# A gated feed-forward layer: the up-projection by a two-by-two Strassen scheme, the down-projection as a stage of its own

## The chip, the cores and the metric

The kernel runs on one core of one Trainium2 chip. The metric is device time in microseconds (us) of one execution, the median of several. The engines are named as in the profile: PE is TensorE (matrix products), PEld its weight load, DVE is VectorE, ACT is ScalarE, POOL is GpSimd, SP is SyncE, which here only issues DMAs; SPq is its queue.

## The reference

One layer of a streaming encoder: a token mixer, a cross-attention into 256 memory tokens and a gated feed-forward network, each with an RMS norm ahead and one behind, added to the residual. There are 2048 prompt rows and 64 sample rows, together T = 2112, and 1024 model columns. All is fp32. The change lies in the feed-forward part:

```python
def conv_ffn(xn, ff_buf, w_up, ffn_conv_w, w_down):
    up, ff_new = causal_dwconv(xn @ w_up, ff_buf, ffn_conv_w)   # width 3 along the rows
    a, g = jnp.split(up, 2, axis=-1)                            # 2 x 2816 columns
    return (jax.nn.gelu(g) * a) @ w_down, ff_new
...
    y = conv_ffn(rms_norm(x, p['norm_ffn_pre']), ff_buf, ...)
    x = x + rms_norm(y, p['norm_ffn_post'])
```

## The kernel before

Every fp32 operand of a product is split into a high part (a rounded copy, written by ScalarE, line 104) and a low part (value minus high part, a subtraction of two operands in SBUF on VectorE, line 105). A product of 128 rows of the contraction is then three matmuls into the same PSUM tile, high by high, high by low and low by high (`mm3`, lines 118 to 120).

The program has four phases. Phases 1 and 2 are the projections and the mixer, phase 3 the attention into the memory; it works through 16 chunks of 128 rows, ends each with a post-norm (`post`) and stores x2, the input of the feed-forward part, to DRAM. Phase 3 ends near 1473 us.

Phase 4 is the feed-forward part. It runs over four `BLOCKS` of rows: three of 512 and one of 512 + 64, which is handled as 2 x 288. In a block, `prep` loads x2, normalizes it and transposes it into SBUF, already split. Then come 22 pairs of up-projection tiles of 128 columns, one for the gate and one for the value: `up_tile` loads a weight tile of 1024 x 128, splits it, and runs 8 x 3 matmuls. VectorE then does the convolution straight from PSUM (lines 1313 to 1320), ScalarE the gelu, VectorE the gating product (line 1336) and the split of the gated rows, which stay in SBUF. The 22 tiles are cut into eight `PARTS`; after the up-projection of a part the down-projection of the part before it runs, its sums kept in SBUF (line 1384). So every weight of the up-projection is loaded and split four times, once per block. At the last part the two stores of the convolution state (`out_ffc`) are issued, and the last post-norms run.

The order of PE's instructions is the order of the code (`manual_schedule`); the order on the other engines is set by a scheduler, except for the tail, where it is written by hand as well. All loads go through SP's queue (`dma`), most stores of inner results through GpSimd's (`store`).

Of the kernel before, what the change touches and what calls it, by code (L numbers as in the profile page):

```python
# [14 lines left out]
P = 128  # L15
# [16 lines left out]
ZB = [("zh", 6144), ("zp", 1024), ("zy0", 1024), ("zy1", 1024), ("zy2", 1024), ("zy3", 1024), ("zy4", 1024),  # L32
      ("zc0", 1024), ("zc1", 1024), ("zc2", 1024), ("zc3", 1024)]
ZA = [("zx", 9216), ("za0", 1024), ("za1", 1024), ("za2", 1024), ("za3", 1024), ("za4", 1024), ("za5", 1024),
      ("za6", 1024)]
# [33 lines left out]
class Prog:  # L69
# [43 lines left out]
    def mm3(self, out, pairs, first=True, last=True):  # L113

        nc = self.nc
        n = len(pairs)
        for i, (lh, ll, rh, rl) in enumerate(pairs):
            nc.tensor.matmul(out, lhsT=lh, rhs=rh, start=(first and i == 0), stop=False)  # L118
            nc.tensor.matmul(out, lhsT=lh, rhs=rl, start=False, stop=False)  # L119
            nc.tensor.matmul(out, lhsT=ll, rhs=rh, start=False, stop=(last and i == n - 1))  # L120
# [17 lines left out]
    def build(self):  # L138
        tc, nc = self.tc, self.nc
        with ExitStack() as es:  # L140
# [21 lines left out]
            self.yaT = dt([4, P, T], F32, name="yaT")  # L162
            self.qT = dt([4, P, T], F32, name="qTd")
# [10 lines left out]
            self.zes = es  # L174
# [5 lines left out]
            self.phase4()  # L180

# [366 lines left out]
    def post(self, pool, halves, gb, xt, dst, w=P, tag="po", yn=None, junk=None, pl=False, hold=None):  # L548
# [9 lines left out]
        for i, h in enumerate(halves):  # L558
            (nc.gpsimd if pl else nc.vector).tensor_tensor(out=yn[:w, cut[i]], in0=h, in1=gb[:w, cut[i]], op=ALU.mult)
# [3 lines left out]
        def finish():  # L563
            for sl in cut:
                if pl:
                    nc.scalar.activation(yn[:w, sl], yn[:w, sl], AF.Copy, scale=r[:w, 0:1])
                    nc.gpsimd.tensor_tensor(out=yn[:w, sl], in0=yn[:w, sl], in1=xt[:w, sl], op=ALU.add)
                else:
                    nc.vector.scalar_tensor_tensor(out=yn[:w, sl], in0=yn[:w, sl], scalar=r[:w, 0:1], in1=xt[:w, sl],
                                                   op0=ALU.mult, op1=ALU.add)  # L570
# [406 lines left out]
    def phase3(self):  # L977
# [4 lines left out]
        zp = self.zp = self.pool(self.zes, "z")  # L982
        bt = [zp.tile([P, n], F32R, tag=t, name="B" + t) for t, n in ZB]
        at = [zp.tile([P, n], F32R, tag=t, name="A" + t) for t, n in ZA]

        def pieces(ts, sizes):
            return [t[:, i:i + D] for t, (_, n) in zip(ts, sizes) for i in range(0, n - D + 1, D)]
        bp, ap = pieces(bt, ZB), pieces(at, ZA)
        A = lambda part, k, sl: ap[part * KT + k][:, sl]
        B = lambda part, k, sl: bp[part * KT + k][:, sl]  # L990
        with ExitStack() as es:
# [67 lines left out]

            wk = self.pool(es, "p3k", side="right")  # L1060
# [16 lines left out]
            def xT(c):  # L1077
# [9 lines left out]
                t = wk.tile([P, 2, KT, P], F32R, tag="xs3", name="xs3", bufs=2)  # L1087
                if c:
                    s.x = wk.tile([P, D], F32, tag="x1", name="x1t", bufs=3)
                    self.dma(s.x, self.x1[c * P:(c + 1) * P])  # L1090
# [30 lines left out]

            def yout(s):
                yos = []
                for nh in range(2):
# [8 lines left out]
                    if nh == 1:  # L1133
                        self.post(wk, yos, self.gb3, s.x, self.x2[s.c * P:(s.c + 1) * P], yn=self.yn3,
                                  junk=s.pp[:, 0:2].rearrange("p h m -> p (h m)"))
                    yield

            self.up0 = []
# [5 lines left out]
            for i in range(16):  # L1144
# [4 lines left out]
                next(g, None)  # L1149
                if i + 2 < 16:  # L1150
                    ch[i + 2] = xT(i + 2)
                if i == 15:
                    for j in (NF, 0):
                        raw = self.raw(a["w_up"][j], (P, KT, P))
                        t = wk.tile([P, 2, KT, P], F32R, tag="xs3", name="up0", bufs=2)
                        self.split(t[:, 0], t[:, 1], raw)
                        self.up0.append((t[:, 0], t[:, 1]))
                if i == 14:
                    self.prep_open()
                    pg = self.prep(0, pt_, "tp")  # L1160
                y = yout(ch[i])
                next(y)
                if i == 15:
                    next(pg)
# [3 lines left out]
                if i >= 14:  # L1168
                    next(pg)
                next(y)  # L1170
                if i >= 14:
                    next(pg)
                if i == 15:
                    next(pg)
                next(y)
                if i == 14:
                    next(pg)
                    next(pg)
                if i == 1:
# [5 lines left out]
                              junk=ch[1].pp[:, 0:2].rearrange("p h m -> p (h m)"))  # L1185


    def prep_open(self):
        nc = self.nc
        zt = lambda t, n, dt=F32: self.zp.tile([P, n], dt, tag=t, name=t + "f")  # L1190
        self.x2s = zt("zx", 9216, F32R).rearrange("p (a k t) -> p a k t", a=2, k=KT)
        self.gpre = zt("za0", D)
        sl = [zt("za%d" % (i + 2), D) for i in range(4)]
        mis = zt("za6", D)
        self.halo = mis[:, 0:88].rearrange("p (j t) -> p j t", t=2)
        self.halos = mis[:, 88:176].rearrange("p (j t) -> p j t", t=2)
        self.ssx = mis[:, 176:240]
        self.flat = mis[:, 240:820]
        ex = zt("za1", D)
        xts = [sl[0], sl[1]]  # L1200
        xns = [sl[2], sl[3], ex]

        def slot(q):
            q.append(q.pop(0))
            return q[-1]

        def xn_slot():
            t = xns.pop(0)
            if t is not ex:
                xns.append(t)  # L1210
            return t
        self.xt_slot = lambda: slot(xts)
        self.xn_slot = xn_slot
        self.dma(self.gpre, self.a["g_ffnpre"].partition_broadcast(P))
        nc.vector.memset(self.halo, 0.0)
        self.dma(self.halos, self.a["sffn"])
        self.pc = 0

    def prep(self, b, pp, tag):

        nc = self.nc
        t0, npr, nsm = BLOCKS[b]
        n = npr + nsm
        xs = self.x2s

        def norm(s):
            w = min(P, n - s)
            xt, xn = self.xt_slot(), self.xn_slot()
            q = 4 * (self.pc % 8)
            self.pc += 1  # L1230
            ss, v, r = (self.ssx[:w, q + i:q + i + 1] for i in range(3))
            self.dma(xt[:w], self.x2[t0 + s:t0 + s + w])
            nc.scalar.activation(xn[:w], xt[:w], AF.Square, accum_out=ss)
            nc.vector.tensor_scalar(out=v, in0=ss, scalar1=1.0 / D, scalar2=EPS, op0=ALU.mult, op1=ALU.add)
            nc.gpsimd.tensor_tensor(out=r, in0=v, in1=self.mhalf[:w, 0:1], op=ALU.pow)
            nc.vector.scalar_tensor_tensor(out=xn[:w], in0=xt[:w], scalar=r, in1=self.gpre[:w], op0=ALU.mult, op1=ALU.mult)
            return xn, s, w
        todo = list(range(0, n, P))
        ready = [norm(todo.pop(0)), norm(todo.pop(0))]
        while ready:  # L1240
            xn, s, w = ready.pop(0)
            for h in range(2):
                tp = pp.tile([P, 4, P], F32, tag=tag, name="tp4")
                for k in range(4):
                    kk = 4 * h + k
                    nc.tensor.transpose(tp[:, k, :w], xn[:w, kk * P:(kk + 1) * P], self.ident[:w, :w])
                qs = slice(4 * h, 4 * h + 4)
                self.split(xs[:, 0, qs, s:s + w], xs[:, 1, qs, s:s + w], tp[:, :, :w])
                if h == 1 and todo:
                    ready.append(norm(todo.pop(0)))  # L1250
                yield

    def phase4(self):
        tc, nc, a = self.tc, self.nc, self.a
        V = nc.vector
        cst = self.cst
        with ExitStack() as es:
            wu = self.pool(es, "p4u", side="right")
            wd = self.pool(es, "p4d", side="right")
            ev = self.pool(es, "p4e", side="right")  # L1260
            xt_slot, xn_slot = self.xt_slot, self.xn_slot
            py = self.pool(es, "p4py", bufs=4, space=PSUM)
            pu = self.pool(es, "p4pu", bufs=4, space=PSUM)
            halo, halos = self.halo, self.halos
# [247 lines left out]
```

## Time and profile before

| | |
|---|---|
| median of 3 runs | 2996.48 us (2992.38 to 3001.1) |
| the profiled execution | 2998.96 us, its span 2997.3 us |
| mean granted TensorE clock | 0.995 |
| PE busy | 2943.8 us, 98% of the span, 15642 matmuls and transposes |
| VectorE busy | 1603.3 us, 53% |
| ScalarE busy | 1142.4 us, 38% |
| GpSimd busy | 242.3 us, 8% |
| chain that ended last | PE 92%, DMA 3%, VectorE 2%, ScalarE 1% |

The times are of whole executions; the span runs from the first to the last instruction that the trace records. The busy share is an average over all stages. The chain is followed back from the last instruction, at each step to what released it.

### The profile page before, as it was taken

What the parts mean: (1) busy time and instruction counts of PE and PEld (TensorE: products, weight loads), DVE (VectorE), ACT (ScalarE), POOL (GpSimd) and SP (SyncE); (2) the same over time, 40 slices, a digit from 0 to 9 for tenths busy, and PEclk for the clock granted to TensorE, in tenths of its full rate; (3) what the DMA queues carried; (4) which work ended last, traced back from release to release, by engine and by line L of the source; (5) the groups of instructions that cost most, each with busy time, mean ns of one, the idle gap of its engine ahead of it and who ended that gap; (6) DMA issues with size and microseconds to landing.
All of it is one profiled execution on the core that took longest, in us unless ns stands there. A gap on an engine that the chain in (4) does not pass through costs nothing.

```text
span 2997.3 us, 40249 instructions
## 1 busy us (share of the span) xinstructions
PE 2943.8 (98%) x15642; PEld 2605.3 (87%) x15642; DVE 1603.3 (53%) x2869; ACT 1142.4 (38%) x2402; POOL 242.3 (8%) x439
## 2 busy tenths in 40 slices
PE   8999999999999999999999999999999999999996
PEld 8999999998888878888788888888888888999995
DVE  6313421446666644333656567665676566655554
ACT  5233223224443432222443344433444334554342
POOL 1111111112212200000000000000000000000001
PEclk9999999999999999999999999999999999999998
DMA  8434332248666421111433235323353233322229
GB/s 275 145 98 134 97 114 88 63 150 297 208 216 194 134 74 60 43 42 50 155 106 106 91 100 162 105 92 106 99 169 107 91 106 102 131 92 85 78 85 54
DMA packets 145457, 352.26 MB, mean 118 GB/s; under 512 B 27094, under 2 KB 64152, under 8 KB 145266
## 3 DMA queue, kind: packets, MB, share of 16 engines
q1 hardware_dynamic: 129730, 299.36, 34.4%
q0 software_dynamic: 15536, 50.33, 4.3%
q8 instruction: 123, 2.02, 0.3%
q14 instruction: 68, 0.56, 0.1%
HBM read 296.60 MB, written 53.03 MB: 117 GB/s over the span
## 4 chain that ended last, share of the span: by engine, by line
PE 92%; DMA 3%; DVE 2%; ACT 1%; issue 1%; POOL 0%; SPq 0%; DVEq 0%; POOLq 0%; ACTq 0%
PE up L118 11%; PE up L120 11%; PE up L119 11%; PE y L118 5%; PE y L119 5%; PE y L120 5%; PE mm L119 4%; PE mm L120 4%; PE mm L118 4%; PE yo L118 3%; PE yo L119 3%; PE yo L120 3%; PE mmb L118 3%; PE mmb L120 3%; PE mmb L119 3%; PE sc L120 2%
## 5 line engine op out<-in xcount | busy, mean ns | idle before, releaser
L118 PE MATMUL up<-zxf,uh 128*128 128x512 f32 (+1 forms) x1744 | 612.0, 351 | 1.3 <-ACT uh L104 1.3
L120 PE MATMUL up<-zxf,ul 128*128 128x512 f32 (+1 forms) x1744 | 611.9, 351 | 0.0
L119 PE MATMUL up<-zxf,uh 128*128 128x512 f32 (+1 forms) x1744 | 611.8, 351 | 0.0
L105 DVE TENSOR_TENSOR ul<-raw,uh 128x1024 fp32r<-128x1024 f32 x174 | 213.1, 1225 | 360.4 <-ACT uh L104 360.4
L118 PEld LDWEIGHTS up<-zxf,uh 128*128 128x128 f32 x1744 | 327.2, 188 | 43.0 <-ACT uh L104 2.2
L120 PEld LDWEIGHTS up<-zxf,ul 128*128 128x128 f32 x1744 | 327.2, 188 | 40.8
L119 PEld LDWEIGHTS up<-zxf,uh 128*128 128x128 f32 x1744 | 327.2, 188 | 40.5
L118 PE MATMUL y<-dh,zhf 128*128 128x512 f32 x680 | 265.5, 390 | 0.0
L120 PE MATMUL y<-dh,zhf 128*128 128x512 f32 x680 | 264.9, 390 | 0.0
L119 PE MATMUL y<-dl,zhf 128*128 128x512 f32 x680 | 264.8, 389 | 0.0
L118 PE MATMUL mm<-xs,wh 128*128 128x384 f32 (+2 forms) x768 | 249.9, 326 | 9.5 <-ACT xs L110 7.4
L104 ACT CAST uh<-raw 128x1024 fp32r<-128x1024 f32 x174 | 183.0, 1052 | 194.5 <-PE up L119 193.5
L120 PE MATMUL mm<-xs,wl 128*128 128x384 f32 (+2 forms) x768 | 249.6, 325 | 0.7 <-DVE wl L105 0.6
L119 PE MATMUL mm<-xs,wh 128*128 128x384 f32 (+2 forms) x768 | 249.9, 326 | 0.0
L118 PE MATMUL mmb<-bh,xs 128*128 128x384 f32 (+1 forms) x512 | 173.4, 339 | 0.0
L120 PE MATMUL mmb<-bh,xs 128*128 128x384 f32 (+1 forms) x512 | 172.5, 337 | 0.0
L119 PE MATMUL mmb<-bl,xs 128*128 128x384 f32 (+1 forms) x512 | 172.4, 337 | 0.0
L104 ACT CAST dh<-raw 128x1024 fp32r<-128x1024 f32 x85 | 87.3, 1049 | 204.1 <-PE y L120 196.6
L118 PEld LDWEIGHTS mm<-xs,wh 128*128 128x128 f32 x768 | 146.4, 191 | 10.4 <-ACT xs L110 7.9
L120 PEld LDWEIGHTS y<-dh,zhf 128*128 128x128 f32 x680 | 127.6, 188 | 26.6
L118 PEld LDWEIGHTS y<-dh,zhf 128*128 128x128 f32 x680 | 127.7, 188 | 26.5 <-ACT za6f L1322 0.3
L119 PEld LDWEIGHTS y<-dl,zhf 128*128 128x128 f32 x680 | 127.7, 188 | 26.0
(514 smaller groups left out, 5537.8 us busy)
## 6 DMA issues: line engine op xcount, KB each, us to landing
raw<-in_w_up SPq DMA_DIRECT2D x176, 512.0 KB, 3.6
raw<-in_w_down SPq DMA_DIRECT2D x88, 512.0 KB, 3.6
raw<-in_wA SPq DMA_DIRECT2D x47, 512.0 KB, 3.7
xt<-in_x SPq DMA_DIRECT2D x32, 512.0 KB, 4.8
kvo_t<-kvo SPq DMA_DIRECT2D x16, 770.0 KB, 5.7
braw<-in_wB SPq DMA_DIRECT2D x64, 192.0 KB, 3.5
x1d<-yn POOLq DMA_DIRECT2D x16, 512.0 KB, 6.1
x2d<-yn POOLq DMA_DIRECT2D x16, 512.0 KB, 5.3
```

The source lines that it names most:

```text
L104: nc.scalar.copy(hi, src)
L105: (eng or nc.vector).tensor_tensor(out=lo, in0=src, in1=hi.bitcast(F32), op=ALU.subtract)
L118: nc.tensor.matmul(out, lhsT=lh, rhs=rh, start=(first and i == 0), stop=False)
L119: nc.tensor.matmul(out, lhsT=lh, rhs=rl, start=False, stop=False)
L120: nc.tensor.matmul(out, lhsT=ll, rhs=rh, start=False, stop=(last and i == n - 1))
```

## The change

The up-projection is computed by Strassen's algorithm in Winograd's form. The contraction (1024) is cut into two halves of four tiles, the rows into pairs of 352 columns of the moving operand (`NB`), and the two output tiles of a pair are the value tile and the gate tile of one f of 22. So phase 4 is now three passes (`NPASS`) of 704 rows, with 22 units each. A unit makes 7 products instead of 8, each of 4 contraction tiles, three matmuls each, 352 columns wide: 84 matmuls. Each weight is loaded three times. The four sums of weight quarters (S1 to S4, lines 1260 to 1265 of the changed kernel) are made on GpSimd, their splits on ScalarE and VectorE; the sums of the row operands (T1 to T4) are made on VectorE, once per pass, and split likewise. What comes out of PSUM is put together on VectorE (u2, u3, cg, ca), and two of the products are accumulated into PSUM tiles whose content has been read out before (`more=True`). The convolution now reads from SBUF, 704 wide.

The gated rows are stored to DRAM (`hd`), and a new phase 5 does the down-projection from there: six `PARTS`, in each all 17 row tiles, with sums of all tiles kept in SBUF. It has as many matmuls as before. The norm and the transposes of x2 are moved from phase 4 into phase 3 (`x2n`, `x2_T`), which stores the transposed rows to DRAM as `x2T`; phase 4 loads them from there. `post` on the last part multiplies by the gain on GpSimd for all tiles but number 15. The core of the diff:

```diff
-BLOCKS = [(0, 512, 0), (512, 512, 0), (1024, 512, 0), (1536, 512, 64)]
-PARTS = [2, 2, 3, 3, 3, 3, 3, 3]
+NB = 352
+NPASS = T // (2 * NB)
+PARTS = [3, 3, 4, 4, 4, 4]
...
-            (nc.gpsimd if pl else nc.vector).tensor_tensor(out=yn[:w, cut[i]], in0=h, in1=gb[:w, cut[i]], op=ALU.mult)
+            (nc.gpsimd if pg else nc.vector).tensor_tensor(out=yn[:w, cut[i]], in0=h, in1=gb[:w, cut[i]], op=ALU.mult)
...
+            def w_s123(u, w):
...
+                a11, a21, a22 = w.r0[:, 0:KH], w.r1[:, 0:KH], w.r1[:, KH:KT]
+                G.tensor_tensor(out=w.s14[:, 0], in0=a21, in1=a22, op=ALU.add)
+                G.tensor_tensor(out=w.s23[:, 0], in0=w.s14[:, 0], in1=a11, op=ALU.subtract)
+                G.tensor_tensor(out=w.s23[:, 1], in0=a11, in1=a21, op=ALU.subtract)
+
+            def w_s4(w):
+                G.tensor_tensor(out=w.s14[:, 1], in0=w.r0[:, KH:KT], in1=w.s23[:, 0], op=ALU.subtract)
...
+            def t_adds(t):
+                V.tensor_tensor(out=t.r["R12"], in0=t.r["R12"], in1=t.r["R11"], op=ALU.subtract)
...
+                V.tensor_tensor(out=t.X, in0=t.r["R22"], in1=t.r["R12"], op=ALU.subtract)
...
+                prod(pa, w.a[:, 0, 0:KH], w.a[:, 1, 0:KH], o["B11"])
+                p1 = vt("p1")
+                nc.scalar.copy(p1, pa[:, :NB])
...
+                if n:
+                    w_s123(u + 1, n)
+                    w_a(u + 1, n)
+                pb = ptile()
+                prod(pb, w.b[:, 0, 0], w.b[:, 1, 0], o["T2"])
+                u2 = vt("u2")
+                V.tensor_tensor(out=u2, in0=pb[:, :NB], in1=p1, op=ALU.add)
...
+                prod(pc, w.b[:, 0, 1], w.b[:, 1, 1], o["T3"])
+                u3 = vt("u3")
+                V.tensor_tensor(out=u3, in0=pc[:, :NB], in1=u2, op=ALU.add)
+                if n:
+                    w_b(u + 1, n)
+                    w_s4(n)
...
+                prod(pa, w.a[:, 0, KH:KT], w.a[:, 1, KH:KT], o["B21"], more=True)
+                ca = cbuf(f, p, "ca")
+                put(ca, p, 0, lambda d, sl: nc.scalar.copy(d, pa[:, sl]))
...
+                prod(pd, w.c[:, 0, 0], w.c[:, 1, 0], o["T1"])
+                cg = cbuf(NF + f, p, "cg")
+                put(cg, p, 1, lambda d, sl: V.tensor_tensor(out=d, in0=pd[:, sl], in1=u3[:, sl], op=ALU.add))
...
+                prod(pe_, w.d[:, 0], w.d[:, 1], o["T4"])
+                put(cg, p, 0, lambda d, sl: V.tensor_tensor(out=d, in0=u3[:, sl], in1=pe_[:, sl], op=ALU.subtract))
...
+                prod(pd, w.c[:, 0, 1], w.c[:, 1, 1], o["B22"], more=True)
+                put(ca, p, 1, lambda d, sl: V.tensor_tensor(out=d, in0=pd[:, sl], in1=u2[:, sl], op=ALU.add))
+                if n:
+                    w_c(n)
...
+                V.tensor_tensor(out=da[:, :e], in0=da[:, :e], in1=dg[:, :e], op=ALU.mult)
...
+                    self.store(self.hd[f, :, t0:t0 + e], da[:, :e])
...
+            self.dma(self.o["ffc"][:, :, 0], halo)
+            self.dma(self.o["ffc"][:, :, 1], halos)
...
+                hr = ld.tile([P, 4, 2 * P], F32, tag="hr", name="hr", bufs=2)
+                self.dma(hr[:, :nf, :n], self.hd[f0:f0 + nf, :, t0:t0 + n].rearrange("f p t -> p f t"))
...
+                    self.split(hh[:, 0, :nf], hh[:, 1, :nf], hr[:, :nf])
```

Three places show how the instructions stand. The first is VectorE in the up-projection, in the steady state. Before, it has this for two column tiles; ul is the low part of a weight tile, up a PSUM tile, zc0f to zc3f the convolution's buffers, zhf the gated rows:

```order
L1314 SCALAR_TENSOR_TENSOR zc1f<-up,cst,zc1f 128x511
L1318 SCALAR_TENSOR_TENSOR zc1f<-za6f,cst,zc1f 128x1
L1316 SCALAR_TENSOR_TENSOR zc1f<-up,cst,zc1f 128x510
L1320 SCALAR_TENSOR_TENSOR zc1f<-za6f,cst,zc1f 128x2
L105 TENSOR_TENSOR ul_13456<-raw,uh_13455 128x1024
L1314 SCALAR_TENSOR_TENSOR zc0f<-up,cst,zc0f 128x511
L1318 SCALAR_TENSOR_TENSOR zc0f<-za6f,cst,zc0f 128x1
L1316 SCALAR_TENSOR_TENSOR zc0f<-up,cst,zc0f 128x510
L1320 SCALAR_TENSOR_TENSOR zc0f<-za6f,cst,zc0f 128x2
L1336 TENSOR_TENSOR zc0f<-zc0f,zc1f 128x512
L105 TENSOR_TENSOR zhf<-zc0f,zhf 128x512
```

In the changed kernel VectorE has this in one unit, from u2 of one unit on; wa to wd are the low parts of the split weights (S2 and S3 in wb, S1 and S4 in wc), s the weight sums, up a PSUM tile, ca and cg the recombined value and gate rows, da and dg the results of the convolution:

```order
L1398 TENSOR_TENSOR u_15021<-up,p_14998 128x352
L1348 SCALAR_TENSOR_TENSOR da<-ca,cst,da 128x704
L1438 TENSOR_TENSOR da<-da,dg 128x704
L1404 TENSOR_TENSOR u_15036<-up,u_15021 128x352
L102 TENSOR_TENSOR wb<-s_15001,wb 128x1024
L102 TENSOR_TENSOR wa<-raw,wa 128x1024
L1418 TENSOR_TENSOR cg<-up,u_15036 128x352
L1423 TENSOR_TENSOR cg<-u_15036,up 128x352
L102 TENSOR_TENSOR wd<-wr_14845,wd 128x512
L1348 SCALAR_TENSOR_TENSOR dg<-cg,cst,dg 128x704
L1431 TENSOR_TENSOR ca<-up,u_15021 128x352
L1348 SCALAR_TENSOR_TENSOR dg<-cg,cst,dg 128x704
```

GpSimd, which had no work of this kind, has this in the same unit (raw and wr are the two loaded weight tiles, halo the two rows that the convolution carries over):

```order
L1262 TENSOR_TENSOR s_14863<-raw,wr_14707 128x512
L1351 COPY halo<-cg 128x2
L1351 COPY halo<-ca 128x2
L1324 COPY cg<-halo 128x2
L1260 TENSOR_TENSOR s_14862<-wr_14707 128x512
L1261 TENSOR_TENSOR s_14863<-s_14862,raw 128x512
L1265 TENSOR_TENSOR s_14862<-raw,s_14863 128x512
L1324 COPY ca<-halo 128x2
L74 DMA hd<-da 128x704
```

What has moved: a unit's low parts and convolution remain on VectorE, the recombination from PSUM is new there, and four sums of 512 columns stand on GpSimd beside them.

The second place is SP's queue where the up-projection ends. Before, the two state stores stand behind all loads of weights, and ahead of the last loads of x2:

```order
L74 DMA raw<-in_w_up 128x1024 x3
L74 DMA raw<-in_w_down 128x1024 x3
L74 DMA out_ffc<-za6f 5632x1x2 x2
L74 DMA out_y<-za4f 64x512 x2
L74 DMA za3f<-x2d 128x1024
L74 DMA out_y<-zy0f 128x512 x2
```

In the changed kernel they stand ahead of the first loads of the gated rows, hr:

```order
L71 DMA raw<-in_w_down 128x1024
L71 DMA wr_22214<-in_w_up 128x1024
L71 DMA raw<-in_w_down 128x1024 x2
L71 DMA out_ffc<-halo 5632x1x2
L71 DMA out_ffc<-halos 5632x1x2
L71 DMA hr<-hd 128x3x256 x2
L71 DMA xt_25182<-x2d 64x1024
```

The same two stores stand now between the two projections instead of ahead of the last post-norms.

The third place is VectorE where phase 3 ends, in the changed kernel (before, the splits of the first weight tiles and of the last chunk's transposes stood here). yn is the result of the last chunk's post-norm, B and T are row operands of the first pass, R and X their unsplit sources:

```order
L566 SCALAR_TENSOR_TENSOR yn_10168<-yn_10168,por,xr 128x512 x2
L102 TENSOR_TENSOR B_13239<-R_13241,B_13239 128x4x352
L93 TENSOR_SCALAR r2v<-ss_13207 128x1
L1299 TENSOR_TENSOR R_13242<-R_13242,R_13241 128x1408
L1121 TENSOR_SCALAR xr<-yn_10168,r2r 128x1024
L1302 TENSOR_TENSOR X<-R_13244,R_13242 128x1408
L102 TENSOR_TENSOR B_13296<-R_13244,B_13296 128x4x352
L1305 TENSOR_TENSOR R_13241<-X,R_13241 128x1408
L102 TENSOR_TENSOR T_13240<-X,T_13240 128x4x352
L102 TENSOR_TENSOR B_13279<-R_13243,B_13279 128x4x352
L102 TENSOR_TENSOR wb<-s_13248,wb 128x1024
L102 TENSOR_TENSOR T_13276<-R_13241,T_13276 128x4x352
```

All of the first pass's operand splits and sums that are not yet done at the last chunk's post-norm stand behind it.

## Rows read from the trace of the kernel before

**Rows 1.** Page: busy time, share of span and instructions of each engine; the final chain.

```profile
PE 2943.8 (98%) x15642; PEld 2605.3 (87%) x15642; DVE 1603.3 (53%) x2869; ACT 1142.4 (38%) x2402; POOL 242.3 (8%) x439
...
PE 92%; DMA 3%; DVE 2%; ACT 1%; issue 1%; POOL 0%; SPq 0%; DVEq 0%; POOLq 0%; ACTq 0%
```

**Rows 2.** PE's groups by shape: count | busy us, mean ns of one | idle before.

```profile
L118 PE MATMUL up<-zxf,uh 128*128 128x512 f32 x1040 | 404.8, 389 | 1.3 <-ACT uh L104 1.3
...
L118 PE MATMUL up<-zxf,uh 128*128 128x288 f32 x704 | 207.2, 294 | 0.0
```

**Rows 3.** PE's waits from 1060 us to the end: total us, times, longest.

```profile
PE tp L1073 <- DMA x1t<-x1d: 1.4, 1, 1.4
PE up L118 <- ACT uh L104: 1.3, 2, 1.1
```

**Rows 4.** Timelines of PE, three stretches: start us, duration us, engine, line, operation.

```profile
1479.77 0.39 PE L118 MATMUL up<-zxf,uh 128*128 128x512 f32 x1
...
1489.97 0.39 PE L118 MATMUL up<-zxf,uh 128*128 128x512 f32 x1
...
99.72 0.33 PE L120 MATMUL mm<-xs,wl 128*128 128x384 f32 x1
...
104.92 0.33 PE L120 MATMUL mm<-xs,wl 128*128 128x384 f32 x1
...
2699.75 0.29 PE L120 MATMUL up<-zxf,ul 128*128 128x288 f32 x1
...
2704.93 0.29 PE L120 MATMUL up<-zxf,ul 128*128 128x288 f32 x1
```

**Rows 5.** VectorE's and ScalarE's groups by shape.

```profile
L105 DVE TENSOR_TENSOR ul<-raw,uh 128x1024 fp32r<-128x1024 f32 x174 | 213.1, 1225 | 360.4 <-ACT uh L104 360.4
...
L1384 DVE TENSOR_TENSOR zy0f<-y,zy0f 128x512 f32<-128x512 f32 x56 | 38.2, 683 | 0.0
...
L331 DVE TENSOR_TENSOR ya<-mm,c 128x384 f32<-128x384 f32 x16 | 8.9, 556 | 9.0 <-PE mm L120 9.0
...
L1306 DVE SCALAR_TENSOR_TENSOR zc0f<-za6f,cst,zc0f 128x578 f32<-128x578 f32 x22 | 18.0, 820 | 4.1 <-ACT zc0f L1304 3.9
...
L104 ACT CAST uh<-raw 128x1024 fp32r<-128x1024 f32 x174 | 183.0, 1052 | 194.5 <-PE up L119 193.5 <-PE up L120 1.0
```

**Rows 6.** Timeline from 1022 to 1033 us, rows of VectorE and GpSimd; releaser in brackets.

```profile
1024.51 4.78 POOL L105 TENSOR_TENSOR zw<-raw,zw 128x1024 fp32r<-128x1024 f32 x2 [4.31 <-PE pA L120]
...
1027.95 2.42 DVE L105 TENSOR_TENSOR lo<-raw,hi 128x1024 fp32r<-128x1024 f32 x1 [0.46 <-ACT hi L104]
...
1030.30 2.82 DVE L111 SCALAR_TENSOR_TENSOR Aza<-pA,cst,Azx 128x256 fp32r<-128x256 f32 x7
...
1030.40 2.40 POOL L105 TENSOR_TENSOR lo<-raw,hi 128x1024 fp32r<-128x1024 f32 x1 [1.10 <-ACT hi L104]
```

**Rows 7.** Timeline from 2925 us to the end: SP's queue, GpSimd, VectorE and PE.

```profile
2934.74 9.44 SPq L74 DMA_DIRECT2D out_ffc<-za6f  x2
...
2959.79 2.54 POOL L559 TENSOR_TENSOR za4f<-za4f,gpost 64x512 f32<-64x512 f32 x2 [373.22 <-ACT za6f L555]
...
2968.03 0.59 SPq L74 DMA_DIRECT2D za3f<-x2d  x1
...
2971.82 0.39 PE L120 MATMUL y<-dz,zhf 128*128 128x512 f32 x1
...
2980.85 1.41 DVE L569 SCALAR_TENSOR_TENSOR zy1f<-zy1f,por,za3f 128x512 f32<-128x512 f32 x2 [9.55 <-DMA za3f<-x2d]
...
2983.64 1.28 DVE L1384 TENSOR_TENSOR zy3f<-y,zy3f 128x512 f32<-128x512 f32 x2
```

**Rows 8.** Windows: us, busy of each engine, granted TensorE clock, DMA share, GB/s.

```profile
1060.00:1080.00 20.00, 17.67 (x86) 14.25 (x85) 8.43 (x14) 9.30 (x17) 1.07 (x2) 1.00 0.44 139
...
2942.00:2966.00 24.00, 24.00 (x108) 19.87 (x107) 13.69 (x23) 6.03 (x14) 4.93 (x5) 1.00 1.91 3
...
24.00:28.00 4.00, 4.00 (x17) 4.00 (x17) 3.85 (x9) 2.99 (x7) 0.00 (x0) 0.59 0.62 170
```

More of the change, by code (lines that the diff above doesn't have):

```diff
@@ L180, in build @@
             self.phase4()
+            self.phase5()
     def phase1(self):
@@ L981, in phase3 @@
         W = NS_TOK
[L982 to L990, printed above, removed]
+        ap = self.pool(self.zes, "za").tile([P, 2, KT, D], F32R, name="A")
+        bp = self.pool(self.zes, "zb").tile([P, 2, KT, D], F32R, name="B")
+        A = lambda part, k, sl: ap[:, part, k, sl]
+        B = lambda part, k, sl: bp[:, part, k, sl]
         with ExitStack() as es:
@@ L1185, in phase3, with x2_T @@
                               junk=ch[1].pp[:, 0:2].rearrange("p h m -> p (h m)"))
-    def prep_open(self):
+                    x2n(yt, xt, W)
+                    todo.append((xt, NP_TOK, W))
+    def x2_T(self, pp, tag, xn, t0, w):
         nc = self.nc
[L1190 to L1251, printed above, removed]
@@ new lines, in phase5 @@
+            es.enter_context(tc.manual_schedule(engines={self.pe}))
+            ac0 = self.pool(es, "p5a")
+            w0 = self.pool(es, "p5w")
+            ac1 = self.pool(es, "p5b")
+            ld = self.pool(es, "p5l", side="right")
+            w1 = self.pool(es, "p5v", side="right")
+            ev = self.pool(es, "p5e", side="right")
+            py = self.pool(es, "p5y", bufs=8, space=PSUM)
+            acc = [(ac0 if j < 6 else ac1).tile([P, D], F32, name="acc%d" % j) for j in range(NT)]
@@ new lines, in phase5, with need @@
+            groups = [NP_TOK] + list(range(0, NP_TOK, 2 * P))
+            f0s = [sum(PARTS[:i]) for i in range(len(PARTS))]
+            work = [(pi, t0) for pi in range(len(PARTS)) for t0 in (groups if pi else groups[1:] + groups[:1])]
+            hs = {}
+            def need(i):
+                if i < len(work) and i not in hs:
+                    pi, t0 = work[i]
+                    hs[i] = load_h(f0s[pi], PARTS[pi], t0)
+            ws = {0: load_down(0, 0, PARTS[0])}
+            need(0)
@@ L1387, in down_part @@
                         if w < P:
-                            fo = xn_slot()
+                            fo = ev.tile([P, D], F32, name="fo5")
                             self.fold(fo[:w], yv)
                             yv = fo
-                        f = self.post(ev, [yv[:w, 0:512], yv[:w, 512:D]], gpost, xt, self.o["y"][t0 + s:t0 + s + w], w=w,
-                                      yn=yv, junk=flat[:, 0:512], pl=tail and w < P, hold=held)
-                        held = [f] if tail else None
@@ L1427 @@
+                        held = [f]
+                if i and work[i - 1][0] != pi:
+                    ws.pop(pi - 1, None)
+            for f in held:
+                f()
 _OUTS = dict(y=(T, D), mk=(KT, P, NM), mv=(KT, P, NM), conv=(P, 4, 2, 2), cn=(P, 2, H, VW), m=(1, 8), ffc=(P, 2 * NF, 2, 2))
```

440 lines of the change are left out of this document (261 added, 179 removed).

## The prediction

> **What bounds the kernel now.** I read the page first, then PE's groups, its waits, its timeline, the other engines' groups, and the rows around the two places where the change puts something new. PE is busy for 98% of the span and makes 92% of the chain that ended last [rows 1], and from 1060 us to the end its longest wait is 1.4 us, the up-projection's waits come to 1.3 us in all [rows 3]: before, the feed-forward part is a stream of matmuls, and everything else in it is hidden. What a change saves in matmuls it therefore gains in full, as long as the other engines keep up; what it makes PE wait, it pays in full. A matmul's duration in the groups (389 ns for 512 columns, 294 for 288 [rows 2]) contains its latency; the spacing of starts counts. From the timelines [rows 4]: 512 columns, 45 gaps in 10.20 us, 0.2267 us each; 384 columns, 30 gaps in 5.20 us, 0.1733; 288 columns, 39 gaps in 5.18 us, 0.1328. On the line between the last two, 352 columns take 0.1328 + 64/96 x 0.0405 = 0.1598 us.
>
> **1. Matmuls.** The code has 3 x 44 x 8 x 3 = 3168 up-projection matmuls of 512 columns before (the trace has 1040 of each line's 1056) and 44 x 2 x 8 x 3 = 2112 of 288: 718 + 280 = 999 us. After: 66 units of 84, 5544 of 352 columns, 886 us. **-113 us.** The down-projection and the transposes stay as many as they were.
>
> **2. What a unit asks of the others.** PE needs 84 x 0.1598 = 13.42 us for a unit. VectorE has, from the order rows, low parts of 1024 columns three times (1.225 us each [rows 5]) and of 512 once (0.68); the convolution, four operations of 704 columns, each by the 820 ns of 578 columns and a slope of 1.06 ns a column (from 683 ns at 512 to 1225 at 1024), 0.95; the gating product of 704, 0.89. That is 3.68 + 0.68 + 3.81 + 0.89 = 9.1 us of operations with two inputs in SBUF. Five of 352 columns read one input from PSUM (556 ns at 384 columns, 0.52 here): 2.6 us. Together 11.7, which alone would fit into 13.42. ScalarE has about as much room: its 1024-column copy takes 1052 ns. GpSimd has four sums of 512 columns. Two operations of 64 x 512 took 2.54 us at the end [rows 7], so 1.27 each, 5.1 a unit, and its copies of two columns beside.
>
> The point is whether VectorE and GpSimd can do this at the same time. In the one stretch where both work on SBUF they can't: two GpSimd subtractions run from 1024.51 to 1029.29 (4.78 us), and VectorE's low part, which starts at 1027.95 and usually takes 1.225 us, takes 2.42 and ends 1.08 us after GpSimd [rows 6]. An operation that reads PSUM and one SBUF operand isn't touched: seven of 256 columns take 2.82 us, 0.40 each, beside a GpSimd subtraction at its usual 2.40 [rows 6]. So a two-input operation waits until GpSimd's instruction is done.
>
> The Trainium skill, in "SBUF — State Buffer", section "Who interferes with whom", has this as an exclusive lock: VectorE and GpSimd share one port pair, and a VectorE operation with two SBUF inputs and a GpSimd operation that reads SBUF block each other fully, whichever comes second. The rows above agree with it (2.42 us for 1.225). Without it the sum would come to the time of the first rival below.
>
> With exclusion a unit takes at least 9.1 + 5.1 = 14.2 us, and, if no sum runs beside a PSUM operation either, 11.7 + 5.1 = 16.8. A sum (1.27 us) is longer than a PSUM operation (0.52), and only the two that make cg stand next to each other in VectorE's order; I let one such pair and one more single operation, 1.56 us, lie beside sums: 16.8 - 1.6 = 15.2 us. PE feels it because the seventh product is added into the PSUM tile that cg is read from, and cg stands on VectorE behind two low parts; so PE stops in each unit. 66 x (15.2 - 13.4) = 117 us, and in the third pass, where the prompt ends inside the columns, two more pieces and copies, about 0.5 us on 22 units, 11. **+128 us**; bounds 66 x 0.8 + 11 = 64 and 66 x 3.4 + 11 = 235.
>
> **3. The two changes of pass.** Row operands are made anew: seven low parts and four sums of 1408 columns on VectorE, 1.225 + 384 x 1.06 ns = 1.63 us each, 18 us. A VectorE that already sets the pace has no room for them, but for what falls into PSUM pieces; 15 each, **+30 us**; bounds 12 (two times what is left of 18 when three or four units with 1.7 us of room take it) and 36.
>
> **4. Phase 3 to phase 4.** The third piece of order shows the same eleven operations, 18 us, queued behind the last chunk's post-norm, which waits for phase 3's last matmul; with the post-norm, three weight low parts, wd and the normalization of x2 VectorE has some 27 us to do before the sixth product can run, and the first unit ends about 31 us after phase 3 instead of 13.4. Four GpSimd sums, 5.1 us, exclude it in part: 35. Of that 2.3 us of waiting is there today [rows 3]. **+20 us**; bounds 10 and 24.
>
> **5. Phase 4 to phase 5.** The two state stores are 5632 pieces of 8 bytes each. SP needs 9.44 us to issue them, from 2934.74; what came behind them in its queue was late: a load issued at 2968.03 was still being waited for until 2980.85, 46 us after the stores began [rows 7]. Over 2942 to 2966 us the DMA engines' records show a share of 1.91, that is, always busy, while moving 3 GB/s [rows 8]. Today this is hidden behind the last products. After, the loads of hr, without which the down-projection can't begin, stand behind them in the same queue. About 2 us after the last product the stores begin, 46 us later hr is there, high and low part take 2 us, and PE, idle that long, starts at half clock: after a gap the granted clock was 0.59 over 4 us [rows 8], 2 us lost. **+52 us**; if the loads weren't held, 2 + 9.4 + 2 + transfer, at least 14. The Trainium skill, in "DMA: Bandwidth & Descriptors", section "Queues, rings and completion order", says that each DMA engine takes the descriptors of one queue in ring order; the 46 us agree. By the page alone the wait has no figure.
>
> **6. Smaller ones.** Phase 3 shares three PSUM tiles with the x2 transposes, some 0.4 us in each chunk, **+5** (0 to 10). In the tail the last matmul starts at 2971.82 and ends at 2972.2, 25.1 us ahead of the end, since loads and stores wait behind the state stores; from the last accumulation (2983.64) to the end it is 13.7 [rows 7], which is what is left: **-11**. Gains on GpSimd in the last part, 2 x 1.27 us a tile, make VectorE's tile (two accumulations, two additions, small ones, 3.1) some 5.6 us against PE's 24 x 0.2267 = 5.44: **+2**.
>
> Sum: -113 + 128 + 30 + 20 + 52 + 5 - 11 + 2 = **+113 us**, against the span of 2997.3: 3110. The execution's own time is 1.7 us above its span (2998.96), and 2.5 above the median of 2996.48. So 3109.5; I say **3110 us**, 3.8% slower.
>
> **Rivals.** *B, the sums are hidden.* Nothing of the exclusion reaches PE: sums fall into PSUM operations and VectorE's gaps, units take 13.4. Then -113 + 12 (pass) + 15 (phase 3 to 4) + 52 + 5 - 11 = -40: 2957 us, faster. It decides as soon as a unit is below 13.42 + 40/66 = 14.0 us. For it: 11.7 leaves 1.7 us of room, and the groups' durations overlap a little from one instruction to the next. Against: 9.1 + 5.1 is above 14.0, and cg stands behind two low parts.
> *C, less in both places.* Only the sum 14.2 counts and hr isn't held (14 instead of 52): -113 + 64 + 30 + 20 + 14 + 5 - 9 = +11, 3007 us; with one of the two, 3046 or 3072. For it: a wait that I read from the tail, where stores were queued too.
> *D, no overlap at all.* 16.8 a unit, +107: 3217 us. For it: sums that are ready late come in front of low parts. That PE falls to half clock in each unit's stop I leave out: 2.3 us of gaps between 1060 and 1080 left the granted clock at 1.00 [rows 8].
>
> **How the numbers follow.** A 0.55, B 0.22, C 0.11, D 0.12. The forecast is A's. A with its bounds reaches from about 3050 to 3170; to leave out two in ten the range takes C, the upper part of B and the lower part of D: 2980 to 3195. A difference of 0.3%, 9 us, is about what a measurement of this kernel can tell. B is faster by more, 0.21 with its upper edge cut off; same 0.05, from the edges of B and C; slower 0.74.
>
> **What would show it.** The spacing of u2 on VectorE gives the unit: 15.2, not 13.4. Low parts and convolution, 1.23 and 0.95 us, should be stretched where they stand beside a GpSimd sum, and PE's waits should name cg on VectorE. Ahead of the first y product PE should stand still for about 50 us, for hr; ahead of the first up product some 20; the tail should be near 14 us. Wrong would make me: u2 every 13.5 us with GpSimd's sums beside PSUM operations, or hr landing some 5 us after its issue.

## The result, and the profile after

The changed kernel takes 3040.97 us (median of 4 runs, 3036.1 to 3042.33) against 2994.43 for the kernel before: 1.015 of it, interval 1.0128 to 1.0173. It is slower, by 46.5 us and not by the 113 of the forecast. The profiled execution has a span of 3040.6 us against 2997.3, 43.3 more; the account below is made against that.

The page of the changed kernel, four of its lines (busy time; PE's busy tenths and the granted clock in 40 slices; last chain), answers to [rows 1]:

```profile
PE 2873.7 (95%) x15906; PEld 2645.1 (87%) x15906; DVE 1856.3 (61%) x2771; ACT 1121.8 (37%) x1979; POOL 1057.6 (35%) x1177
...
PE   8999999999999999999689998999899957999998
...
PEclk9999999999999999999899998999899978999999
...
PE 45%; DVE 12%; issue 5%; ACT 2%; SPq 1%; DMA 1%; POOL 0%; DVEq 0%; ACTq 0%; POOLq 0%
```

PE is busy for 70 us less, yet the whole is longer: PE now stands still in places, the clock dips in nearly the same slices, and PE makes 45% of the last chain instead of 92%. Its waits from 1400 us to the end (answer to [rows 3]: total, times, longest):

```profile
PE y L115 <- ACT dh L101: 54.2, 1, 54.2
PE up L115 <- DVE cg L1418: 39.5, 28, 8.0
PE up L115 <- ACT wb L101: 9.7, 1, 9.7
PE tp L1184 <- DVE xr L1121: 6.9, 1, 6.9
PE up L115 <- ACT B L101: 3.0, 1, 3.0
PE up L116 <- DVE B L102: 3.0, 1, 3.0
```

One wait of 54 us stands ahead of the first y product. Its row names dh, the split of the first down weights, which stands behind hh, the split of hr, in ScalarE's queue; the section between the projections shows that hr came last. Another 39.5 us of waits for cg are spread over 28 places. If each of the 66 units had waited for cg as the forecast had it, this would be over 100.

**Where the units are.** Each unit has one u2 on VectorE. Four of them in the timeline of VectorE, those of the 21st, 27th, 43rd and 49th unit:

```profile
1802.36 0.52 DVE L1398 TENSOR_TENSOR u<-up,p 128x352 f32<-128x352 f32 x1
...
1905.46 0.52 DVE L1398 TENSOR_TENSOR u<-up,p 128x352 f32<-128x352 f32 x1 [0.51 <-PE up L117]
...
2123.46 0.52 DVE L1398 TENSOR_TENSOR u<-up,p 128x352 f32<-128x352 f32 x1 [0.33 <-PE up L117]
...
2224.56 0.51 DVE L1398 TENSOR_TENSOR u<-up,p 128x352 f32<-128x352 f32 x1
```

Between the second and third lie 16 units, 13.63 us each, not 15.2. Between first and second, and third and fourth, lie six units each with a change of pass: 103.1 and 101.1 us. Two windows of PE, PEld, VectorE, ScalarE and GpSimd (busy us, granted clock, DMA share, GB/s) show the steady state, the first those 16 units of the second pass, the second 16 units of the third:

```profile
1905.46:2123.46 218.00, 217.92 (x1346) 215.52 (x1345) 205.26 (x225) 109.30 (x144) 173.32 (x145) 1.00 0.30 104
2224.56:2451.30 226.74, 220.15 (x1346) 215.58 (x1346) 217.30 (x258) 110.91 (x144) 190.39 (x225) 1.00 0.28 98
```

In the second pass PE does not stop, at full clock, and VectorE is busy 12.83 us a unit; in the third it is 13.58, and a unit takes 14.17. So the sums fit almost exactly into VectorE's room. Exclusion is there all the same. VectorE and GpSimd in one unit of the second pass, from their timeline:

```profile
1944.09 1.21 DVE L102 TENSOR_TENSOR wc<-s,wc 128x1024 fp32r<-128x1024 f32 x1
1944.32 1.02 POOL L1324 COPY cg<-halo 128x2 f32<-128x2 f32 x1
1945.22 0.94 DVE L1348 SCALAR_TENSOR_TENSOR da<-ca,cst,da 128x704 f32<-128x704 f32 x1
1945.38 1.93 POOL L1260 TENSOR_TENSOR s<-wr 128x512 f32<-128x512 f32 x1
1946.22 0.52 DVE L1398 TENSOR_TENSOR u<-up,p 128x352 f32<-128x352 f32 x1
1946.66 1.40 DVE L1348 SCALAR_TENSOR_TENSOR da<-ca,cst,da 128x704 f32<-128x704 f32 x1
1947.39 1.82 POOL L1261 TENSOR_TENSOR s<-s,raw 128x512 f32<-128x512 f32 x1
1948.10 1.87 DVE L1438 TENSOR_TENSOR da<-da,dg 128x704 f32<-128x704 f32 x1
```

The copy of two columns takes 1.02 us and ends with wc; the sum that starts at 1945.38 is held until the convolution's step ends, runs beside u2, which reads PSUM and keeps its 0.52 us, and holds the next step up, which takes 1.40 for 0.95; the product after it takes 1.87 for 0.89. Both sides wait. In this pass neither wait reaches PE, which is busy for 217.92 of the 218.00 us.

**Between the projections.** SP's queue and the operations that wait for it, from the timeline, where the up-projection's last matmul starts at 2473.15 and the first y product at 2527.71:

```profile
2475.39 0.63 SPq L71 DMA_DIRECT2D out_ffc<-halo  x1
...
2476.07 8.13 SPq L71 DMA_DIRECT2D out_ffc<-halos  x1
...
2484.37 26.17 SPq L71 DMA_DIRECT2D hr<-hd  x2
...
2523.71 0.83 ACT L101 CAST hh<-hr 128x768 fp32r<-128x768 f32 x1 [46.79 <-DMA hr<-hd]
```

The loads of hr are issued behind 11264 pieces, and the queue takes 26 us to accept two of them; hr is there 48.3 us after the stores began (46 in [rows 7]). The windows there show the granted clock at 0.50 while PE stands still, and still at 0.64 from 2530 to 2535 us, after PE has started again at 2527.71:

```profile
2500.00:2520.00 20.00, 0.00 (x0) 0.00 (x0) 0.00 (x0) 0.00 (x0) 0.00 (x0) 0.50 1.21 15
...
2530.00:2535.00 5.00, 5.00 (x16) 3.97 (x15) 1.83 (x3) 1.54 (x2) 0.00 (x0) 0.64 0.98 314
```

The tail is short, as forecast: the last matmul ends at 3030.1, 10.5 us ahead of the end (25.1 in [rows 7]).

### The profile page after: what moved, and what is told of

It reads as the page before. It is cut to its first block, busy times and chain, and to the rows that moved or that the text cites. A ratio compares the mean times of both kernels' runs of the same rounds, so it can differ in the third digit from the quotient of the medians.

```text
span 3040.6 us, 41676 instructions
## 1 busy us (share of the span) xinstructions
PE 2873.7 (95%) x15906; PEld 2645.1 (87%) x15906; DVE 1856.3 (61%) x2771; ACT 1121.8 (37%) x1979; POOL 1057.6 (35%) x1177
## 4 chain that ended last, share of the span: by engine, by line
PE 45%; DVE 12%; issue 5%; ACT 2%; SPq 1%; DMA 1%; POOL 0%; DVEq 0%; ACTq 0%; POOLq 0%
PE up L115 6%; PE up L116 6%; PE up L117 6%; PE y L116 4%; PE y L117 4%; PE y L115 4%; DVE da L1348 2%; PE yo L116 2%; PE yo L117 2%; PE yo L115 2%; PE sc L117 2%; PE sc L115 2%; PE sc L116 2%; DVE acc L566 1%; SPq L71 1%
## 5 line engine op out<-in xcount | busy, mean ns | idle before, releaser
L115 PE MATMUL y<-dh,hh 128*128 128x512 f32 x704 | 275.0, 391 | 54.2 <-ACT dh L101 54.2
L116 PE MATMUL y<-dl,hh 128*128 128x512 f32 x704 | 275.0, 391 | 0.5 <-DVE dl L102 0.5
L117 PE MATMUL y<-dh,hh 128*128 128x512 f32 x704 | 274.9, 390 | 0.0
L1534 DVE TENSOR_TENSOR acc<-y,acc 128x512 f32<-128x512 f32 x170 | 115.5, 689 | 181.2 <-PE y L117 180.4
L115 PEld LDWEIGHTS y<-dh,hh 128*128 128x128 f32 x704 | 132.8, 189 | 82.2 <-ACT dh L101 54.5
L115 PE MATMUL up<-T,wb 128*128 128x352 f32 x528 | 172.6, 327 | 9.7 <-ACT wb L101 9.7
L1348 DVE SCALAR_TENSOR_TENSOR da<-ca,cst,da 128x704 f32<-128x704 f32 (+1 forms) x132 | 174.5, 1322 | 9.1 <-ACT da L1346 9.0
L115 PE MATMUL up<-B,wa 128*128 128x352 f32 x528 | 174.5, 330 | 3.0 <-ACT B L101 3.0
L116 PE MATMUL up<-B,wa 128*128 128x352 f32 x528 | 172.6, 327 | 3.0 <-DVE B L102 3.0
L117 PE MATMUL up<-B,wa 128*128 128x352 f32 x528 | 172.6, 327 | 0.0
L117 PE MATMUL up<-T,wb 128*128 128x352 f32 x528 | 171.0, 324 | 1.7 <-DVE wb L102 1.7
L116 PE MATMUL up<-T,wb 128*128 128x352 f32 x528 | 170.9, 324 | 0.0
L101 ACT CAST hh<-hr 128x1024 fp32r<-128x1024 f32 (+3 forms) x54 | 49.5, 916 | 311.3 <-PE y L117 262.1
L116 PEld LDWEIGHTS y<-dl,hh 128*128 128x128 f32 x704 | 132.6, 188 | 28.5 <-DVE dl L102 1.2
L117 PEld LDWEIGHTS y<-dh,hh 128*128 128x128 f32 x704 | 132.7, 189 | 27.9 <-DVE hh L102 0.5
```

The costliest lines, as they stand in the source:

```text
L101: nc.scalar.copy(hi, src)
L1348: V.scalar_tensor_tensor(out=d[:, :e], in0=c[:, i:e + i], scalar=w[i], in1=d[:, :e], op0=ALU.mult, op1=ALU.add)
L1534: V.tensor_tensor(out=acc[j][:, sl], in0=pt, in1=acc[j][:, sl], op=ALU.add)
```

## The experiments

Theory: the exclusion is real but falls mostly on GpSimd, so that the steady units cost little; the 113 us of saved matmul time went into four stops, namely the start of phase 4, the two changes of pass and the loads of hr. Rival: the prediction's, that the exclusion sets the pace in each unit. The changed kernel itself is taken as 1.015 of the runs of before beside each experiment, some 3036.6 us for the first four and 3034 for the next four. The interval of that ratio, 1.0128 to 1.0173, leaves each gain against the changed kernel uncertain by about 7 us either way.

**One store for the state.**

```diff
-            self.dma(self.o["ffc"][:, :, 0], halo)
-            self.dma(self.o["ffc"][:, :, 1], halos)
+            nc.scalar.copy(both[:, :, 0], halo)
+            nc.scalar.copy(both[:, :, 1], halos)
+            self.dma(self.o["ffc"], both)
```

> The two state stores of 5632 pieces of 8 bytes are replaced by two small copies into one tile and one store of 128 pieces of 704 bytes, at the same place. Theory (the loads of hr are held behind the pieces in SP's queue): the 54 us stop ahead of the first y product falls to some 15 us, time 3041 - 39 = about 3002 us. Rival (the stop is the way of the last gated rows through DRAM, store and load, whatever lies ahead in the queue): stop and time unchanged, 3041 us.

Measured: 2993.59 us, 1.0009 of before (0.9999 to 1.0018), 43 us less than the changed kernel. Its PE waits:

```profile
PE up L115 <- DVE cg L1419: 39.0, 27, 7.8
PE y L115 <- ACT dh L101: 9.9, 1, 9.9
```

The 54.2 us are 9.9, while the wait for cg has not changed. The stop came from the small pieces; without them the way through DRAM costs 10 us, less than the 15 that I allowed. That it was the order in SP's queue and not the load on the DMA engines is not shown: the edit takes both away, and with the pieces the last 320 KB store of gated rows, which goes through GpSimd's queue, landed 21.7 us after its issue, against a median of 3.2 in the whole run.

**The sums on VectorE.** In the four lines of the weight sums:

```diff
-                G.tensor_tensor(out=w.s14[:, 0], in0=a21, in1=a22, op=ALU.add)
+                V.tensor_tensor(out=w.s14[:, 0], in0=a21, in1=a22, op=ALU.add)
```

> The four weight sums of a unit run on VectorE instead of GpSimd. Theory (exclusion is real, but only a part of the four sums is paid for): VectorE's own starts take 10.7 us a unit, the sums add 4 x 0.62 = 2.5, 13.2 in all, no stretched operations; units at 13.4 to 13.6 in passes 1 and 2, pass 3 no slower than its 14.15, time within 20 us of 3041. Rival of the prediction (exclusion sets the pace): units shorter by 1 us or more, below 2990 us.

Measured: 2997.64 us, 1.0019 (1.0009 to 1.0028), 39 us less. The units are where the theory had them, but the gain is twice what it allowed and not far from the rival's. PE's waits for cg are 21.3 us in 6 places instead of 39.5 in 28. Where the gain lies is read from the units (windows over 16 units of the second and of the third pass):

```profile
1886.95:2101.86 214.91, 214.91 (x1340) 214.88 (x1339) 207.01 (x290) 111.55 (x144) 58.88 (x81) 1.00 0.30 106
2196.69:2412.59 215.90, 215.90 (x1346) 215.90 (x1345) 209.28 (x322) 109.98 (x145) 120.80 (x161) 1.00 0.30 103
```

13.43 and 13.49 us a unit, with PE never stopping: 0.2 and 0.68 us less. Over the six units around a change of pass it takes 97.1 and 94.8 us where the changed kernel takes 103.1 and 101.1, and over the first four units 55.3 for 62.8. So having the sums on GpSimd instead of VectorE costs about 37 us: 11 in the 16 units of the third pass, 6 in 32 units of the others, 12 at the changes of pass, 8 at the start. This is not the exclusion alone: a sum also takes 0.68 us on VectorE and 1.27 on GpSimd.

**No row operands for passes 2 and 3.** The blocks under `if last:`, the two sums ahead of them and the loads of the next pass are left out:

```diff
-                last = f == NF - 1 and p + 1 < NPASS
-                if f == 3 and p + 1 < NPASS:
-                    nt = t_load(p + 1)
-                if f == NF - 2 and p + 1 < NPASS:
-                    t_adds(nt)
+                last = False
```

> Passes 2 and 3 reuse the row operands of the first pass: loads, sums and splits of the row operands at the two changes of pass are left out, so the output of those rows is not the layer's. Theory (the eleven operations of 1408 columns are what the change of pass costs): the two stops go, 20 + 17 = 37 us, time about 3004 us; everything else stays. Rival (the stop is a clock or a weight buffer matter at the end of the pass): less than 10 us.

Measured: 2993.01 us, 1.0007 (0.9998 to 1.0017), 44 us less. In place of 39.5 us in 28 waits for cg this stands:

```profile
PE up L115 <- DVE cg L1414: 9.2, 21, 0.9
```

What is left is the third pass's 0.4 us a unit. So the long waits for cg were the operands of the next pass: in the changed kernel the two changes cost 22 and 20 us, of which 16 and 14 would be there with the sums on VectorE, by the run before. Without the operands the six units take 81.8 and 84.9 us, 21 and 16 less, the 37 of the theory. Another 7 us lie in the first four units, 55.8 us instead of 62.8. There the changed kernel's VectorE already makes two sums for the second pass, beside the work of the first:

```profile
1536.77 2.70 DVE L1299 TENSOR_TENSOR R<-R,R 128x1408 f32<-128x1408 f32 x1
...
1545.37 1.61 DVE L1302 TENSOR_TENSOR X<-R,R 128x1408 f32<-128x1408 f32 x1
```

**No sums at all.** Only the first unit's sums are made (the same return stands in `w_s4`):

```diff
             def w_s123(u, w):
-                if u == 0:
-                    w.s14, w.s23 = s14, s23
-                else:
-                    w.s14 = early.tile([P, 2, KH, P], F32, tag="s14", name="s14", bufs=1)
-                    w.s23 = early.tile([P, 2, KH, P], F32, tag="s23", name="s23", bufs=1)
+                w.s14, w.s23 = s14, s23
+                if u:
+                    return
```

> The four weight sums are made for the first unit alone and reused by all others, so GpSimd has only its small copies and stores; the output is not the layer's. Theory: units go to 13.45 in all passes, which is 4 + 4 + 16 us, and the changes of pass get a few us cheaper; about 3005 to 3015 us. Rival of the prediction (exclusion is the main loss): below 2960 us.

Measured: 2984.24 us, 0.9976 (0.9967 to 0.9986), 52 us less: more than the theory said, much less than the rival. Sixteen units of the second pass:

```profile
1873.53:2089.43 215.90, 215.90 (x1346) 215.90 (x1345) 176.67 (x226) 111.17 (x144) 53.49 (x80) 1.00 0.30 105
```

A unit is 13.49 us, all PE: 0.1606 us a matmul. VectorE is busy 11.04 us in it. With the sums on GpSimd it was 12.83, so of their 5.1 us VectorE paid 1.8. The two operations that pay most, without the sums and with them (16 units of the second pass each; count, then busy us and mean ns):

```profile
L102 DVE TENSOR_TENSOR wb<-s,wb 128x1024 fp32r<-128x1024 f32 x16 | 19.6, 1225 | 3.0 <-ACT wb L101 3.0
L1439 DVE TENSOR_TENSOR da<-da,dg 128x704 f32<-128x704 f32 x16 | 14.3, 892 | 0.5
...
L102 DVE TENSOR_TENSOR wb<-s,wb 128x1024 fp32r<-128x1024 f32 x16 | 30.0, 1876 | 0.0
L1438 DVE TENSOR_TENSOR da<-da,dg 128x704 f32<-128x704 f32 x16 | 29.9, 1868 | 0.5
```

The 52 us (about 7 either way) are all that the sums cost in the changed kernel, and only 16 of them lie in the steady units. Over the six units of a change of pass it takes 88.6 and 89.2 us, 26 less in all, and over the first four 51.2, 12 less.

**Both edits.** The store joined and the sums on VectorE.

> Both edits together: one store of 704-byte pieces for the state, and the weight sums on VectorE. Alone they gave 43 and 39 us against the changed kernel's 1.015 of before. Theory (two different stops, one behind SP's queue and one from the exclusion): they add, 2992 x 1.015 - 43 - 39 = about 2955 us, faster than before. Rival (both free the same idle time): 2990 us.

Measured: 2955.51 us, 0.9886 (0.9871 to 0.99). They add, as expected: the two stops are not the same time.

**And the last transposes later.** In phase 3, besides (the lines that give chunk 15 its residual from the tile already loaded are left out here):

```diff
-                while todo:
+                while todo and i < 15:
                     self.x2_T(pt_, "tp", *todo.pop(0))
...
                 next(y)
                 next(y)
+                while todo:
+                    self.x2_T(pt_, "tp", *todo.pop(0))
                 if i + 1 < 16:
                     pT(ch[i + 1])
```

> As the run before, and the transposes of x2 of chunk 14 stand behind half of chunk 15's last products instead of ahead of them, with chunk 15's residual taken from the tile that is there already. Theory (PE stands still for 7.0 us for the normalized rows of chunk 14): 7 us less than the run before, about 2948 us. Rival (the stop moves on to the first up product, which waits for the same post-norms): no gain.

Measured: 2946.58 us, 0.9854 (0.9839 to 0.9868), 9 us less than both edits; the stop for xr is 1.5 us instead of 6.9 and none took its place. The u2 of the first unit comes 7.8 us earlier. This is the fastest version, 1.5% below the kernel before. Its largest waits:

```profile
PE up L115 <- DVE cg L1426: 21.9, 6, 6.4
PE y L115 <- DVE hh L102: 9.6, 1, 9.6
PE up L115 <- ACT wb L101: 7.5, 1, 7.5
```

**One row operand for the first pass.** The other six splits and the four sums of the first pass are left out:

```diff
+            for n in ("T2", "T3", "B21", "T1", "T4", "B22"):
+                tk.o[n] = tk.o["B11"]
```

> The changed kernel, with one row operand split for the first pass and used in all seven products; the other six splits and the four sums of the first pass are left out, so the first 704 rows are not the layer's. Theory (behind phase 3 the queue of operand splits on VectorE is what holds PE): some 25 of the 35 us of stops in the first two units go, 3037 - 25 = about 3012 us. Rival (the stops wait for loads or for the last post-norm): less than 10 us.

Measured: 3015.62 us, 1.0086 (1.0071 to 1.0101), some 19 us less. From phase 3's last matmul to the u2 of the fifth unit it takes 84.8 us where the changed kernel takes 96.2, so only 11.4 of the 19 lie at the start; 8 lie at the first change of pass. Neither side's number came: the operands are a third of the start's stops. PE's waits there, 1480 to 1600 us, in this run:

```profile
PE up L115 <- DVE cg L1413: 5.5, 3, 2.9
PE up L115 <- ACT wb L101: 4.3, 1, 4.3
PE up L115 <- ACT B L101: 3.0, 1, 3.0
```

What it waits for then is cg in three places, and the first weight split and the first operand, which stand behind the post-norm; from 1490 to 1500 us the granted clock is 0.56. How these share the rest is open.

**The kernel before with one store.** The same edit of the store in the kernel before:

> The kernel before, with the state stores joined into one of 704-byte pieces and nothing else. Theory (its tail of 25.1 us is the hold-up of SP's queue behind the pieces): the tail falls to about 13 us, 11 to 12 us off, 2980 us. Rival (the tail is the last post-norms' own length): unchanged.

Measured: 2986.97 us, 0.999 (0.998 to 0.9999): 2.4 us, not 11. Its tail is 15.8 us, so the mechanism is there, but the time does not follow the 25.1 us of [rows 7]. Two more profiles of the kernel before and a second run of the edit ask why:

> The kernel before, unchanged, for a second profile beside the run of the joined store: that run gained 2 to 3 us where 11 to 12 were expected. Theory (what the pieces hold up in the tail differs from execution to execution, and the first profile was a long one): the tail from the last matmul to the end is shorter than 25.1 us here, near 16 to 20. Rival (the tail is always 25, and the joined store lost 9 us elsewhere): 25 us again, and the phases ahead shorter than with the joined store.

> The same, a third profile of the kernel before; the same two theories.

> The kernel before with one joined store, again beside the kernel before. Theory: the ratio is 0.999 again within 0.001, the tail 15.8 us again. Rival (a chance of the chip): 0.996, as the first profile's tail would have it.

The two executions of the kernel before took 2991.57 and 2989.12 us, their spans 2989.9 and 2987.4. The first one's last matmul and the wait behind it (answer to [rows 7]):

```profile
2968.89 0.39 PE L120 MATMUL y<-dz,zhf 128*128 128x512 f32 x1
...
2973.45 1.41 DVE L569 SCALAR_TENSOR_TENSOR zy1f<-zy1f,por,za3f 128x512 f32<-128x512 f32 x2 [5.09 <-DMA za3f<-x2d]
```

The tail is 2989.9 - 2969.3 = 20.6 us, and 20.5 in the other, where the wait is 5.04 us instead of 9.55. The edit's second run is 0.9984 (0.9975 to 0.9994), 2984.23 us against 2988.85, with 15.8 us of tail and this wait:

```profile
2965.79 1.41 DVE L569 SCALAR_TENSOR_TENSOR zy1f<-zy1f,por,za3f 128x512 f32<-128x512 f32 x2 [0.34 <-DMA za3f<-x2d]
```

So the pieces cost the kernel before 2 to 5 us, and its first profile was of an execution with a long tail. The best version stands at about 0.987 even against the kernel before with this edit (0.9854 / 0.9987, the mean of the two ratios).

## Why the prediction was right in direction and wrong in size

Term by term, against the 43.3 us between the two profiled spans:

| term | forecast | measured | from |
|---|---|---|---|
| matmuls | -113 | -108 | 5544 x 0.1606 (units without sums) against 999 |
| units, exclusion | +128 | +16 | 0.13 us in passes 1 and 2, 0.68 in pass 3 |
| two changes of pass | +30 | +42 | 103.1 and 101.1 less 6 x 13.49 each |
| phase 3 to 4 | +20 | +43 | u2 of the first unit 33.4 us after phase 3's last matmul starts, 4.1 if nothing waited; the next four units 8.8 too long; 7.0 for xr; less 1.3 of before and 0.9 of moved transposes |
| phase 4 to 5 | +52 | +56 | 54.4, and 2 at half clock |
| phase 3 | +5 | about +10 | its last matmul starts at 1488.3 us instead of 1460.3, 27.9 later, less 10.6 of moved transposes (twelve groups of eight, 0.88 us each by starts) and 7.0 counted above |
| tail | -9 | -15 | 10.5 against 25.1 |
| sum | +113 | +44 | |

Two of my readings of before were wrong. Phase 3's last matmul starts at 1460.3 us, not near 1473. And of the waits of [rows 3] only the 1.3 us for uh lie between phases 3 and 4, not 2.3; the 1.4 for x1t stand where phase 3 begins.

**The step that failed is step 2**, the unit's price, 128 us for 16. That the two engines exclude each other was right, and so was the list of the operations that do, 9.1 + 5.1 us. Wrong was that their sum sets the pace of a unit, so that PE stops in each. First, the sum added durations, where the starts of queued operations lie some 0.06 us closer: VectorE's 11.7 us are 11.04. Second, I let 1.6 us of the 5.1 lie beside operations from PSUM or in gaps, and it was 3.3. GpSimd's sums take 1.73 to 1.93 us in the second pass instead of 1.27, so most of the waiting is theirs, and PE does not wait for them there. Third, VectorE therefore has 11.04 + 1.8 = 12.83 us of work in a unit, which stays below PE's 13.49, where my 15.2 stood above it. My lower bound of 14.2 us was above the measured 13.63, so the range of this term did not hold its value. The condition of rival B, a unit below 14.0 us, came true in two passes of three; the kernel is slower all the same because B's stops were too cheap.

**The direction was luck.** With 16 in place of 128 my own sum is +1, no change. The kernel is slower because the stops between the stages cost some 40 us more than I gave them, and that is not what the forecast rested on.

**Steps 3 and 4 were right in mechanism and too small.** A change of pass costs 21 us instead of 15, and the start 43 instead of 20. By the run with the sums on VectorE, their place on GpSimd makes 6 of each change and 8 of the start. At the start three things were not in the forecast at all: the stop of 7.0 us for xr ahead of the last chunk's products, the two sums of the second pass (7 us, by the run without them), and the clock. I had counted half clock for one stop alone. In the changed kernel, at the start and at the first change of pass:

```profile
1490.00:1500.00 10.00, 4.02 (x12) 3.33 (x12) 9.05 (x12) 6.01 (x7) 6.76 (x7) 0.66 0.34 138
...
1510.00:1520.00 10.00, 9.01 (x41) 9.01 (x42) 10.00 (x7) 2.24 (x3) 6.15 (x3) 0.68 0.75 216
...
1830.00:1840.00 10.00, 8.47 (x37) 8.47 (x38) 9.87 (x11) 5.37 (x6) 3.93 (x3) 0.64 0.78 253
```

In the last window, 37 matmuls take 8.47 us where 0.1606 each would be 5.9, so 2.5 us are lost behind the stop itself. At the start, where the clock is at 0.66 from 1490 to 1530 us, the starts of matmuls that waited for nothing lie 7 us further apart in all than at 0.1606 each. These shares overlap in part and are not a sum.

**Steps 1 and 5 held.** The spacing for 352 columns (0.1598 for 0.1606) was read off two other widths, and the hold-up of hr came within 4 us; the edit that takes the pieces away shows that it is theirs. Step 6 gave phase 3 +5 and it was about +10: PE's waits from 1060 to 1470 us are 5.7 us instead of 2.4, and the rest was not traced. The tail's size rested on one execution: with 20.5 us, as in the two other profiles of the kernel before, this term would be -10.

Rival D's 16.8 us a unit did not come: units take 13.6 to 14.2. Nor did the third pass's short stops lower the clock, which is 1.00 in its window. Rival C's shorter wait for hr came only when the pieces were gone.

The Trainium skill, in "SBUF — State Buffer", section "Who interferes with whom", says that of a VectorE operation with two SBUF inputs and a GpSimd operation that reads SBUF the second to start blocks fully. The rows above agree, on both sides: a step of the convolution takes 1.40 us for 0.95, a sum 1.93 for 1.27.

## What to carry to other kernels

Two engines that exclude each other cost the time only what reaches the engine that bounds. Here the sums took 5.1 us a unit, VectorE paid 1.8 of it and had 2.4 us of room, and a unit grew by 0.13 us in two passes. In the third, where VectorE's 13.58 us lay above PE's 13.49, it grew by 0.68. So add up the busy time of the engine that shares, from starts and not from durations, compare it with the pace of the engine that bounds, and if it stays below, look first at the places where the load is higher for one unit. How far this carries when the sums are much longer no run here shows. A saving in the bounding engine can be given back where the stages meet, since there operands are remade, queues are drained and the clock falls. Here four such places took about 140 us, and the algorithm saved 108. Look at every store of many small pieces that a change moves ahead of a load that something needs.

## What the runs showed of the hardware that was not expected

Behind two stores of 5632 pieces of 8 bytes PE stood still for 50.1 to 54.2 us between the projections (the five profiled executions that have them there). The first load behind them was in use 44.2 to 48.3 us after the first store was issued; in the tail of the kernel before, where most of this is hidden behind products, it was 46.1, 41.7 and 41.6 us in three executions, and the wait that was left 9.55, 5.09 and 5.04. One store of 128 pieces of 704 bytes with the same content landed in 1.6 us. GpSimd's copies of two columns, 0.18 us when free, took 1.00 and 1.18 us on average in 16 units of the second pass, ahead of cg and of ca; the timeline above shows one that ends with VectorE's low part.
